# Memory rows transposed unscaled, and cached log gates loaded 64 keys to a partition

## The chip, the cores and the metric

One Trainium2 chip, one core of it. The kernel is one launch; its time is device microseconds (us) from start to end. Three runs give 1922.89, 1914.52 and 1916.93, median 1916.93. Engines by the names of the profile: PE is TensorE (matmuls), PEld its weight loads, DVE VectorE, ACT ScalarE, POOL GpSimd, SP SyncE, which issues all the transfers spoken of here.

## The reference

One step of a layer for 1,024 prompt frames and 8 decode streams of 16 new frames each, with 1,024 cached keys a stream. Three token mixers run side by side (stick-breaking attention, SSD, forgetting attention "fox"), then cross-attention into 256 memory rows and an FFN. The change touches two pieces:

```
def mem_kv(mem, g, wk, wv):
    mn = rmsnorm(mem, g)                       # mem (256, 1024): row * rsqrt(mean square) * gain of the column
    k = einsum('bmd,de->bme', mn, wk)          # 1024 x 1024, likewise v with wv
# forgetting attention of the decode streams
logf = log_sigmoid(fg + fox_b_f)               # gates of the new rows, 4 heads
fcum = cumsum(concat([past['fox_logf'], logf], axis=1), axis=1)    # past: (8, 1024, 4)
s = s + (fcum of the query - fcum of the key)  # added to the scores before the softmax
```

`p_mem_k`, `p_mem_v`, the new gates `p_fox_logf`, `s_fox_logf` and the outputs of the layer are returned.

## The kernel before

All large products are f32 by three passes: an operand is split into a high part (a cast on ACT, `split_into`) and a low part (the difference, usually on POOL in pieces of 256 columns, L132), and `mm3` (L325 to L328) adds high x high, high x low and low x high.

**Order of the work.** One program order per engine is fixed when the kernel is built: a scheduler simulates the engines and places each instruction where its operands would be ready, and `keep_in_program_order` pins some. On the chip each engine runs its list in that order and waits at an instruction whose operand is late; what stands behind it on that engine waits too. SP issues the transfers in such a list.

**Start.** L140 to L148 load the memory rows `xm` (two halves of 128 rows), five rows of gains and the convolution taps, and the first two blocks of `wk_x`. `norm_T` (L259 to L278) squares the rows on ACT (L265), takes the root (`rstd_of`), scales the rows in place on DVE (L269), transposes them on TensorE (L275) and copies the transposes out, with the gain of the column, as high (ACT, L276) and low part (DVE, L277). `mem_proj` then runs 16 units, each 256 rows of `wk_x` or `wv_x` by 512 columns: `w_unit` loads the block (L315), splits it (ACT cast L290, POOL L132), two units ahead; 12 products per unit (two row halves, two k tiles, three passes). After four units the sums go from PSUM to SBUF (ACT copy) and are stored twice (L835). Between the units a helper `aux` norms and transposes the prompt frames (loads L437, the same `norm_T` lines), whose products with `w_in` come next.

**`fox_sums`.** Lies some 280 us in, in the stream of filling work between attention units. It makes the new gates `lf` (a chain of small DVE instructions, L402 to L409, then L660), stores them (L662, L663), loads the cached gates with key p of each 128 on partition p (L666), sums the prompt's gates along the keys with a triangular matrix (L678, L679) and does the same for the cached gates: block sums on DVE (L693 to L696), 15 products with `triu` and `ones` into rows of (stream, head) (L708, L710), ACT copies, the new rows' sums behind them (L713 to L717). The rows go to a scratch `fs_sc` in DRAM, written twice (L718). Each of the four fox decode units later loads its gate rows from there, spread over the partitions (`fkb`, L909), and L1246 loads the column of the new rows.

Around `fox_sums` stand a decode unit of stick-breaking attention (key loads L882, their transposes L888, the weights made on POOL L132 and transposed at L925) and the blocks of `w_in` for the z and xBC columns (L315, cast L290, splits L132).

## Time and profile before

| what | value |
|---|---|
| median of three runs | 1916.93 us |
| profiled execution | 1915.89 us, span 1914.2 us |
| granted TensorE clock, mean | 0.988 |
| TensorE busy | 1837.6 us, 96% |
| DVE, ACT, POOL busy | 897.1, 823.7, 622.6 us |
| packets below 512 B | 89996 of 309742 |

A row of busy time adds up the time in which an engine worked; the span less TensorE's busy time is what TensorE stood. In a list of waits the line is that of the waiting instruction, behind "<-" stands what released it. In a timeline a row is: start and duration in us, engine, line, operation, tiles out and in, shapes, count, and in brackets the idle time of the engine ahead of it with its releaser. "clock" is the share of full speed that TensorE was granted.

### The profile page before, as it was taken

To read this page: it belongs to the slowest core of one execution; us is meant where nothing else is said; L and a number is where in the kernel's file an instruction comes from. 1 tells how busy PE (TensorE), PEld (TensorE's weight loads), DVE (VectorE), ACT (ScalarE), POOL (GpSimd) and SP (SyncE) were. 2 spreads that over 40 slices of the span, in tenths; PEclk is the share of its full clock that TensorE was granted. 3 is DMA by queue.
4 is the path that set the end of the run, shared out by engine and by line. 5 is a ranking of instruction groups with operands and counts; after the bars stand their busy time and mean duration, and the time that the engine had idled before them with its cause. 6 is when DMAs were issued, how large, how long until landed. Compare 5 with 4: busy or idle time off the path is not lost. (4 is left out here: it accounts for less than half of the span.)

```text
span 1914.2 us, 32508 instructions
## 1 busy us (share of the span) xinstructions
PE 1837.6 (96%) x12146; PEld 1641.4 (86%) x12146; DVE 897.1 (47%) x1823; ACT 823.7 (43%) x1782; POOL 622.6 (33%) x921
## 2 busy tenths in 40 slices
PE   7989989999998889999999999999999999999998
PEld 5889877888876667898998889999999999888886
DVE  3421323457646873353445387333333433455554
ACT  6431534545566771243433275333333333344443
POOL 7532416254324563211102205544444443000000
PEclk9999998999999999999999999999999999999999
DMA  9455645536579887244558124322323223567572
GB/s 336 142 165 159 211 115 152 154 109 185 166 220 282 280 290 260 103 150 145 176 194 291 66 91 111 80 70 70 95 74 75 70 70 100 190 194 237 177 246 92
DMA packets 309742, 305.70 MB, mean 160 GB/s; under 512 B 89996, under 2 KB 261108, under 8 KB 309584
## 3 DMA queue, kind: packets, MB, share of 16 engines
q1 hardware_dynamic: 309584, 303.62, 51.6%
q8 instruction: 96, 1.57, 0.3%
q14 instruction: 62, 0.51, 0.1%
HBM read 229.31 MB, written 74.24 MB: 159 GB/s over the span
## 5 line engine op out<-in xcount | busy, mean ns | idle before, releaser
L132 POOL TENSOR_TENSOR wl<-wr,wh 128x256 fp32r<-128x256 f32 (+2 forms) x184 | 138.6, 787 | 222.4 <-ACT wh L290 202.0
L326 PE MATMUL psd<-act,wh 128*128 128x384 f32 x576 | 198.7, 345 | 5.1 <-DVE sg L453 2.7
L327 PE MATMUL psd<-act,wh 128*128 128x384 f32 x576 | 197.6, 343 | 0.0
L328 PE MATMUL psd<-act,wl 128*128 128x384 f32 x576 | 196.8, 342 | 0.7 <-POOL wl L132 0.7
L1849 PE MATMUL pst<-bT,tr 128*128 128x256 f32 (+1 forms) x1068 | 155.0, 293 | 0.0
L1849 PEld LDWEIGHTS pst<-bT,tr 128*128 128x128 f32 x1068 | 144.9, 188 | 0.1
L328 PE MATMUL psd<-wh,act 128*128 128x512 f32 (+3 forms) x424 | 135.8, 322 | 0.0
L326 PE MATMUL psd<-wh,act 128*128 128x256 f32 (+3 forms) x414 | 133.0, 324 | 2.4 <-ACT pt L1445 1.2
L1849 PE MATMUL psd<-bT,tr 128*128 128x320 f32 (+1 forms) x912 | 133.2, 295 | 0.8 <-DVE tr L1693 0.5
L327 PE MATMUL psd<-wl,act 128*128 128x256 f32 (+3 forms) x414 | 132.8, 322 | 0.5 <-POOL wl L132 0.5
L1849 PEld LDWEIGHTS psd<-bT,tr 128*128 128x128 f32 x912 | 124.7, 188 | 1.8 <-DVE tr L1693 0.7
L326 PEld LDWEIGHTS psd<-act,wh 128*128 128x128 f32 x576 | 109.1, 189 | 8.7 <-DVE sg L453 3.1
L132 POOL TENSOR_TENSOR tr<-u,tr 128x256 fp32r<-128x256 f32 x110 | 81.9, 774 | 102.3 <-ACT tr L1689 85.1
L328 PEld LDWEIGHTS psd<-act,wl 128*128 128x128 f32 x576 | 108.9, 189 | 2.3 <-POOL wl L132 1.0
L327 PEld LDWEIGHTS psd<-act,wh 128*128 128x128 f32 x576 | 109.0, 189 | 1.5 <-issue 1.1
L132 POOL TENSOR_TENSOR ws<-ws 128x256 f32<-128x256 f32 (+2 forms) x100 | 68.5, 713 | 115.3 <-DVE ws L519 99.9
L1824 DVE TENSOR_TENSOR tr<-tr,pst 128x256 f32<-128x256 f32 (+1 forms) x86 | 38.6, 449 | 139.5 <-ACT tr L1821 106.3
L251 POOL TENSOR_SCALAR sm<-sm 128x1 f32<-128x1 f32 (+2 forms) x27 | 7.1, 261 | 296.6 <-ACT y L1932 208.0
L132 POOL TENSOR_TENSOR tr<-raw,tr 128x256 fp32r<-128x256 f32 x94 | 69.2, 765 | 84.5 <-ACT tr L1689 76.3
L1689 ACT CAST tr<-tr 128x384 fp32r<-128x384 f32 (+1 forms) x70 | 37.7, 538 | 121.1 <-DMA tr<-hidsc 104.3
L290 ACT CAST wh<-wr 128x512 fp32r<-128x512 f32 (+2 forms) x90 | 52.2, 621 | 80.7 <-PE psd L328 31.0
L326 PEld LDWEIGHTS psd<-wh,act 128*128 128x128 f32 x414 | 78.3, 189 | 9.9 <-ACT pt L1445 1.5
(620 smaller groups left out, 4714.0 us busy)
## 6 DMA issues: line engine op xcount, KB each, us to landing
u<-w_down SPq DMA_DIRECT2D x40, 512.0 KB
raw<-w_down SPq DMA_DIRECT2D x26, 512.0 KB
st<-qksc SPq DMA_DIRECT2D x48, 256.0 KB
wr<-w_in SPq DMA_DIRECT2D x44, 256.0 KB
tr<-hidsc SPq DMA_DIRECT2D x57, 192.0 KB
hidsc<-tr SPq DMA_DIRECT2D x34, 288.0 KB
qksc<-sg SPq DMA_DIRECT2D x48, 192.0 KB
wr<-cache_sb_k SPq DMA_DIRECT2D x32, 256.0 KB
```

What stands on the lines that cost most here:

```text
L132: POOL.tensor_tensor(out=out[:, a0:a1], in0=in0[:, a0:a1], in1=in1[:, a0:a1], op=op)
L251: POOL.tensor_scalar(v, ss, inv, EPS, ALU.mult, ALU.add)
L290: ACT.copy(hi, raw)
L326: PE.matmul(out, ah, bh, start=start, stop=False)
L327: PE.matmul(out, ah, bl, start=False, stop=False)
L328: PE.matmul(out, al, bh, start=False, stop=stop)
L1689: ACT.copy(hi, src)
L1824: DVE.tensor_tensor(out=at(out, g), in0=at(x, g), in1=ps[g][:, :GW[g]], op=op)
L1849: PE.matmul(dst[g][:, :GW[g]], x[:, ka], y[:, k, :], start=start and k == 0 and m == 0, stop=stop and k == 3 and m == 2, skip_group_check= ...
```

## The change

Three edits.

1. *Memory rows.* The rows are transposed as loaded; the copies out of PSUM apply only the gain. The squares and the root follow after the first unit (`root`), and the root of a memory row is applied when the products are copied out (scale `rstd[0]`, kept in `xm_r`). The loads are reordered: first half of the rows, five gain rows, second half, four blocks of `wk_x`, then the taps, which get their own transpose after the second unit (`tap_columns`). Weight blocks are loaded four units ahead, split two ahead as before; the low parts of 7 of 16 units (0, 1, 2, 5, 8, 11, 14) are made on DVE in one instruction, the others on POOL.
2. *Cached gates.* The load puts 64 consecutive keys of one stream on a partition (16 partitions a stream), all heads together: 128 runs of 1 KB where there were 8,192 of 16 bytes. Four scans on DVE, one a head, sum within a partition; one small product with a constant matrix `before` adds the partitions ahead of it. `fs_sc` is now (head, stream, key), written once; the sums of the new rows go to `fn_sc`.
3. *Gate rows.* Each fox decode unit loads its rows `fkb` by two transfers, one a stream.

On TensorE the instructions of the start come in another order. What stands in its list (`pst`, `psd`: PSUM tiles; `xc`: gain rows; `act`: memory rows and their transposes; `wh`, `wl`: high and low parts of the weights), before:

```order
L219 MATMUL pst<-ident,xc 128x72
L275 MATMUL pst<-ident,act 128x128 x6
L326 MATMUL psd<-wh,act 128x512
L327 MATMUL psd<-wl,act 128x512
L326 MATMUL psd<-wh,act 128x512
L327 MATMUL psd<-wl,act 128x512
L275 MATMUL pst<-ident,act 128x128 x2
```

and now:

```order
L226 MATMUL pst<-ident,xc 128x40
L843 MATMUL pst<-ident,act 128x128 x12
L340 MATMUL psd<-wh,act 128x512 x2
L341 MATMUL psd<-wl,act 128x512
L342 MATMUL psd<-wh,act 128x512
L340 MATMUL psd<-wh,act 128x512
L341 MATMUL psd<-wl,act 128x512
```

Twelve of the sixteen transposes stand ahead of the first product, where six did.

On SP, the loads of the start (`ws`: prompt frames; `hb`: small constants; `wr`: blocks of `w_in`; `st`: blocks of `wk_x`), before:

```order
L315 DMA st<-wk_x 128x2x512
L437 DMA ws<-x_prompt 128x1024 x3
L1220 DMA hb<-fox_b_f 128x4
L1221 DMA hb<-dt_bias 128x8
L1222 DMA hb<-a_log 128x8
L1223 DMA hb<-d_skip 128x8
L437 DMA ws<-x_prompt 128x1024 x4
L315 DMA wr<-w_in 128x4x128
L315 DMA st<-wk_x 128x2x512 x5
```

and now:

```order
L147 DMA st<-wk_x 128x2x512 x4
L156 DMA xc<-conv_w 32x128
L861 DMA st<-wk_x 128x2x512
L451 DMA ws<-x_prompt 128x1024 x3
L1265 DMA hb<-fox_b_f 128x4
L1266 DMA hb<-dt_bias 128x8
L1267 DMA hb<-a_log 128x8
L1268 DMA hb<-d_skip 128x8
L451 DMA ws<-x_prompt 128x1024 x4
L329 DMA wr<-w_in 128x4x128 x4
L861 DMA st<-wk_x 128x2x512 x3
```

Five blocks of `wk_x` go out ahead of the frames, where three did, and four blocks of `w_in` ahead of the sixth block, where one did.

On SP at `fox_sums` (`sg`: cached gates; `lf`: new gates), before:

```order
L666 DMA sg<-cache_fox_logf 128x64x4
L882 DMA wr<-cache_sb_k 128x512 x2
L608 DMA mixsc<-sg 64x2x256
L882 DMA wr<-cache_sb_k 128x512 x2
L662 DMA p_fox_logf<-lf 128x8x4
L663 DMA s_fox_logf<-lf 128x4
L315 DMA wr<-w_in 128x2x256
```

and now:

```order
L681 DMA sg<-cache_fox_logf 128x256
L927 DMA wr<-cache_sb_k 128x512 x2
L622 DMA mixsc<-sg 64x2x256
L927 DMA wr<-cache_sb_k 128x512 x2
L329 DMA wr<-w_in 128x2x256
L329 DMA wr<-w_in 128x2x8
L329 DMA wr<-w_in 128x2x256
L329 DMA wr<-w_in 128x2x8
L329 DMA wr<-w_in 128x2x256
L329 DMA wr<-w_in 128x2x8
L329 DMA wr<-w_in 128x2x256
L676 DMA p_fox_logf<-lf 128x8x4
L677 DMA s_fox_logf<-lf 128x4
L329 DMA wr<-w_in 128x2x8
```

The stores of `lf` moved behind seven of the eight `w_in` pieces. On DVE the four scans (L712) stand directly ahead of the first instruction of the chain that ends in `lf` (L416, before L402). Elsewhere the lists of all engines are as they were, but for the two loads of `fkb`.

The diff, cut to its core:

```diff
-    xm = act_t(F32)
-    for i in range(2):
+    xm, rows = act_t(F32), xc_t()
+    first_raw = []
+    def load_xm(i):
         SP.dma_start(out=xm[:, i * D:(i + 1) * D], in_=a["mem_prompt"][0, i * P:(i + 1) * P, :])
-    rows = xc_t()
+    def load_wk(n):
+        first_raw.append(st_t(F32))
+        SP.dma_start(out=first_raw[-1].rearrange("p (k n) -> p k n", n=512),
+                     in_=a["wk_x"][0][2 * n * P:(2 * n + 2) * P, 0:512].rearrange("(k p) n -> p k n", p=P))
+    load_xm(0)
     for i, g in enumerate(("norm_mix_g", "norm_x_g", "norm_ffn_g", "mem_norm_g", "conv_b")):
         SP.dma_start(out=rows[8 * i:8 * i + 8, :P], in_=a[g][0].rearrange("(k p) -> k p", p=P))
-    SP.dma_start(out=rows[40:72, :P], in_=a["conv_w"][0].rearrange("i (k p) -> (i k) p", p=P))
-    first_raw = []
-    for k0 in (0, 2):
-        first_raw.append(st_t(F32))
-        SP.dma_start(out=first_raw[-1].rearrange("p (k n) -> p k n", n=512),
-                     in_=a["wk_x"][0][k0 * P:(k0 + 2) * P, 0:512].rearrange("(k p) n -> p k n", p=P))
+    load_xm(1)
+    for n in range(4):
+        load_wk(n)
+    SP.dma_start(out=rows[64:96, :P], in_=a["conv_w"][0].rearrange("i (k p) -> (i k) p", p=P))
...
     colp = pT()
-    PE.transpose(colp[:, :72], rows[:72, :P], ident[:72, :72])
+    PE.transpose(colp[:, :40], rows[:40, :P], ident[:40, :40])
     cols = cst.tile([P, 72], F32, name="cols")
-    DVE.tensor_copy(cols, colp[:, :72])
-    DVE.tensor_scalar(cols[:, 32:72], cols[:, 32:72], 0.5, None, ALU.mult)
+    DVE.tensor_copy(cols[:, 0:40], colp[:, :40])
+    def tap_columns():
+        tp = pT()
+        PE.transpose(tp[:, :32], rows[64:96, :P], ident[64:96, 64:96])
+        DVE.tensor_copy(cols[:, 40:72], tp[:, :32])
+        DVE.tensor_scalar(cols[:, 32:72], cols[:, 32:72], 0.5, None, ALU.mult)
     g_mix, g_x, g_ffn, g_mem = (cols[:, 8 * i:8 * i + 8] for i in range(4))
...
     hb = mcst.tile([P, 28], F32, name="hb")
+    xm_r = mcst.tile([P, 2], F32, name="xm_r")
     lf = mcst.tile([P, NBLK, 4], F32, name="lf")
...
     fc_sc = dram([4, SEQ], F32, "fcsc")
-    fs_sc = dram([32, 2, PAST + DEC_S], F32, "fssc")
+    fs_sc = dram([4, DEC_B, PAST], F32, "fssc")
+    fn_sc = dram([32, DEC_S], F32, "fnsc")
     ac_sc = dram([72, P], F32, "acsc")
...
-    def split_unit(raw, n):
+    def split_unit(raw, n, eng=POOL):
         hi, lo = unit_pair()
-        split_into(hi[:, :n], lo[:, :n], raw[:, :n])
+        split_into(hi[:, :n], lo[:, :n], raw[:, :n], eng)
         return hi, lo
...
-        pl0, pl1 = sg_t(), sg_t()
-        SP.dma_start(out=pl0[:, :256].rearrange("p (u h) -> p u h", h=4),
-                     in_=a["cache_fox_logf"][0].rearrange("b k h -> (b k) h").rearrange("(u p) h -> p u h", p=P))
-        triu, ones = pl1[:, 256:384], pl1[:, 384:512]
-        POOL.memset(pl1[:, 256:], 1.0)
+        lp, tri = sg_t(), sg_t()
+        SP.dma_start(out=lp[:, :256], in_=a["cache_fox_logf"][0].rearrange("b (c k) h -> (b c) (k h)", k=64))
+        triu, ones, before = (tri[:, i * P:(i + 1) * P] for i in range(3))
+        POOL.memset(tri[:, :384], 1.0)
         POOL.affine_select(out=triu, in_=triu, compare_op=ALU.is_ge, fill=0.0, base=0, pattern=[[1, P]],
                            channel_multiplier=-1)
+        b3 = before.rearrange("p (b t) -> p b t", t=16)
+        POOL.affine_select(out=b3, in_=b3, compare_op=ALU.is_ge, fill=0.0, base=-1, pattern=[[16, 8], [1, 16]],
+                           channel_multiplier=-1)
+        POOL.affine_select(out=b3, in_=b3, compare_op=ALU.is_ge, fill=0.0, base=0, pattern=[[-16, 8], [0, 16]],
+                           channel_multiplier=1)
...
         DVE.tensor_copy(fqc.rearrange("p b h -> p (b h)"), tp[:, :32])
-        pp, ps_ = pl1[:, :256], pl0[:, 256:]
-        DVE.tensor_copy(pp.rearrange("p (k b h) -> p k b h", k=8, h=4),
-                        pl0[:, :256].rearrange("p (b k h) -> p k b h", k=8, h=4))
         yield
...
         SP.dma_start(out=fc_sc, in_=fr[0:4, :SEQ])
-        DVE.tensor_copy(ps_[:, 32:64], pp[:, 0:32])
-        for k in range(1, 7):
-            sl = slice(32 * k, 32 * k + 32)
-            DVE.tensor_tensor(out=ps_[:, 32 * k + 32:32 * k + 64], in0=ps_[:, sl], in1=pp[:, sl], op=ALU.add)
-        x8 = sg2_t()
-        DVE.tensor_tensor(out=x8[:, :32].rearrange("p (b h) -> p b h", h=4),
-                          in0=lf[:, 8, :].unsqueeze(1).to_broadcast([P, 8, 4]),
-                          in1=smask.unsqueeze(2).to_broadcast([P, 8, 4]), op=ALU.mult)
+        for hd in range(4):
+            x = lp[:, hd:256:4]
+            DVE.tensor_tensor_scan(lp[:, 256 + 64 * hd:320 + 64 * hd], x, x, 0.0, ALU.add, ALU.bypass)
+        tot = pre[:, 32:36]
+        DVE.tensor_copy(tot, lp[:, 319:512:64])
+        x8, t8 = pre[:, 64:96], pre[:, 96:128]
+        for out, src in ((x8, lf[:, 8, :]), (t8, tot)):
+            DVE.tensor_tensor(out=out.rearrange("p (b h) -> p b h", h=4), in0=src.unsqueeze(1).to_broadcast([P, 8, 4]),
+                              in1=smask.unsqueeze(2).to_broadcast([P, 8, 4]), op=ALU.mult)
         yield
-        sr = xc_t()[0:32, :PAST + DEC_S]
-        for hf in range(2):
-            tp = pd()
-            for k in range(4 * hf, 4 * hf + 4):
-                o = tp[:32, (k % 4) * P:(k % 4 + 1) * P]
-                PE.matmul(o, pp[:, k * 32:(k + 1) * 32], triu, start=True, stop=k == 0)
-                if k:
-                    PE.matmul(o, ps_[:, k * 32:(k + 1) * 32], ones, start=False, stop=True)
-            ACT.copy(sr[:, hf * 512:(hf + 1) * 512], tp[:32])
         tp = pd()
-        PE.matmul(tp[:32, :16], x8[:, :32], fold, start=True, stop=True)
-        ACT.copy(x8[0:32, 64:80], tp[:32, :16])
-        n8 = x8[0:32, 64:80]
+        PE.matmul(tp[:, :4], before, tot, start=True, stop=True)
+        PE.matmul(tp[:32, 16:32], x8, fold, start=True, stop=True)
+        PE.matmul(tp[:32, 32:48], t8, ones[:, :16], start=True, stop=True)
+        DVE.tensor_tensor(out=lp[:, 256:512].rearrange("p (h k) -> p h k", h=4),
+                          in0=lp[:, 256:512].rearrange("p (h k) -> p h k", h=4),
+                          in1=tp[:, 0:4].unsqueeze(2).to_broadcast([P, 4, 64]), op=ALU.add)
+        n8 = pre[0:32, 128:144]
+        DVE.tensor_copy(n8, tp[:32, 16:32])
         DVE.tensor_tensor_scan(n8, n8, n8, 0.0, ALU.add, ALU.bypass)
-        DVE.tensor_scalar(sr[:, PAST:], n8, sr[:, PAST - 1:PAST], None, ALU.add)
-        SP.dma_start(out=fs_sc, in_=sr.unsqueeze(1).to_broadcast([32, 2, PAST + DEC_S]))
+        DVE.tensor_tensor(out=n8, in0=n8, in1=tp[:32, 32:48], op=ALU.add)
+        SP.dma_start(out=fs_sc.rearrange("h b (c k) -> (b c) h k", k=64),
+                     in_=lp[:, 256:512].rearrange("p (h k) -> p h k", h=4))
+        SP.dma_start(out=fn_sc, in_=n8)
         yield
...
         DVE.tensor_tensor(out=y8[0:32, :P].rearrange("p (b t) -> p b t", t=DEC_S),
-                          in0=sr[:, PAST:].unsqueeze(1).to_broadcast([32, 8, DEC_S]),
+                          in0=n8.unsqueeze(1).to_broadcast([32, 8, DEC_S]),
                           in1=bmask32.unsqueeze(2).to_broadcast([32, 8, DEC_S]), op=ALU.mult)
...
         mh, ml = act_pair(256)
-        drain(norm_T([xm[:, i * D:(i + 1) * D] for i in range(2)], g_mem, lambda: (mh, ml), 256, xm[:, 2 * D:]))
         work = [(a[wname][0], j, k0, sc, out) for wname, sc, out in (("wk_x", mk_sc, "p_mem_k"), ("wv_x", mv_sc, "p_mem_v"))
                 for j in range(2) for k0 in (0, 2, 4, 6)]
-        nxt = [[t[:, :1024].rearrange("p (k n) -> p k n", n=512) for t in split_unit(raw, 1024)] for raw in first_raw]
+        def unit(n):
+            return [t[:, :1024].rearrange("p (k n) -> p k n", n=512)
+                    for t in split_unit(first_raw.pop(0), 1024, DVE if n < 2 or n % 3 == 2 else POOL)]
+        nxt = [unit(0)]
+        for k in range(KT):
+            tp = pT()
+            for i in range(2):
+                PE.transpose(tp[:, i * P:(i + 1) * P], xm[:, i * D + k * P:i * D + (k + 1) * P], ident)
+            ACT.activation(mh[:, k, :], tp[:, :256], AF.Copy, scale=g_mem[:, k:k + 1])
+            DVE.scalar_tensor_tensor(ml[:, k, :], tp[:, :256], g_mem[:, k:k + 1], f32(mh[:, k, :]), ALU.mult, ALU.subtract)
+        nxt.append(unit(1))
+        ss, rstd = small(2), []
+        def root():
+            for i in range(2):
+                tc.keep_in_program_order(ACT.activation(xm[:, 2 * D:], xm[:, i * D:(i + 1) * D], AF.Square,
+                                                        accum_out=ss[:, i:i + 1]))
+            r = xm_r[:, 0:2]
+            DVE.tensor_copy(r, rstd_of(ss, 2, 1.0 / D))
+            rstd.append(r)
         for n, (w, j, k0, sc, out) in enumerate(work):
             wh, wl = nxt.pop(0)
-            if n + 2 < len(work) :
-                w2, j2, k2 = work[n + 2][:3]
-                nxt.append(w_unit([(w2, j2 * 512, 512)], k2, 2, st_t(F32)))
+            if n + 4 < len(work):
+                w2, j2, k2 = work[n + 4][:3]
+                first_raw.append(st_t(F32))
+                SP.dma_start(out=first_raw[-1].rearrange("p (k n) -> p k n", n=512),
+                             in_=w2[k2 * P:(k2 + 2) * P, j2 * 512:(j2 + 1) * 512].rearrange("(k p) n -> p k n", p=P))
+            if n + 2 < len(work):
+                nxt.append(unit(n + 2))
             if k0 == 0:
...
                     t = sg_t()
-                    ACT.copy(t, ps[i])
+                    ACT.activation(t, ps[i], AF.Copy, scale=rstd[0][:, i:i + 1])
                     for dst in (sc, a[out][0, 0].rearrange("m h d -> m (h d)")):
                         SP.dma_start(out=dst[i * P:(i + 1) * P, j * 512:(j + 1) * 512], in_=t)
+            if n == 0:
+                root()
+            if n == 1:
+                tap_columns()
             next(aux, None)
...
             fkb = xc_t()
-            SP.dma_start(out=fkb[:, :PAST],
-                         in_=fs_sc[8 * p:8 * p + 8, :, :PAST].rearrange("i c k -> (i c) k").unsqueeze(1)
-                         .to_broadcast([16, DEC_S // 2, PAST]))
+            for b2 in range(2):
+                SP.dma_start(out=fkb[64 * b2:64 * b2 + 64, :PAST],
+                             in_=fs_sc[:, 2 * p + b2, :].unsqueeze(1).to_broadcast([4, DEC_S, PAST]))
             return fox_rows(T, pieces, [(0, PAST, fkb[:, :PAST]), (PAST, P, fnew)], fqs[:, p:p + 1]), hold
...
                     tc.keep_in_program_order(
-                        SP.dma_start(out=fqs[:, p:p + 1], in_=fs_sc[8 * p:8 * p + 8, 0, PAST:PAST + DEC_S]))
+                        SP.dma_start(out=fqs[:, p:p + 1], in_=fn_sc[8 * p:8 * p + 8, :]))
             if o[0] == "z":
...
             elif o == "dt":
```

## The prediction

> **What bounds the kernel now.** I read the page's busy shares first, then its chain, then TensorE's waits, and last the timeline and stretches around the two longest.
>
> ```profile
> span 1914.2 us, 32508 instructions
> PE 1837.6 (96%) x12146; PEld 1641.4 (86%) x12146; DVE 897.1 (47%) x1823; ACT 823.7 (43%) x1782; POOL 622.6 (33%) x921
> PE 45%; DVE 1%; issue 0%; POOL 0%; ACT 0%; DVEq 0%; POOLq 0%
> ```
>
> TensorE is busy for 96% of the span; 76.6 us are idle. So only two things shorten the run: fewer products, or a shorter stop of TensorE. The chain says the same (DVE, POOL and ACT have a hundredth or less of the span). The profiled execution took 1915.89 us, 1.7 more than its span and 1.0 less than the median of the three runs (1916.93); sums below start from 1915.9, and I leave the 1.0 out, as the three runs lie 8.4 apart.
>
> The waits of TensorE (line, for whom; total us, times, longest):
>
> ```profile
> PE pst L219 <- DMA xc<-conv_w: 7.0, 1, 7.0
> PE pst L888 <- DMA wr<-cache_sb_k: 5.8, 4, 4.9
> PE pst L925 <- POOL ws L132: 3.5, 1, 3.5
> PE pst L275 <- DVE act L277: 1.2, 2, 0.9
> PE psd L327 <- POOL wl L132: 0.5, 1, 0.5
> ```
>
> The first, fourth and fifth lie in the memory projection at the start, the second and third around `fox_sums`. Stretches of those two places (us, then busy us of PE, PEld, DVE, ACT, POOL; clock granted to TensorE, DMA share, GB/s):
>
> ```profile
> 0.00:10.00 10.00, 0.37 (x2) 0.20 (x2) 6.05 (x37) 4.78 (x7) 4.99 (x21) 1.00 0.75 253
> 17.00:34.00 17.00, 15.81 (x82) 12.33 (x81) 8.97 (x18) 11.77 (x22) 9.14 (x15) 1.00 1.07 375
> 280.00:285.00 5.00, 0.09 (x5) 0.03 (x1) 3.47 (x20) 1.09 (x2) 0.60 (x2) 0.73 1.03 130
> 285.00:292.50 7.50, 6.95 (x32) 6.07 (x33) 1.28 (x10) 2.36 (x5) 0.00 (x0) 0.50 0.81 153
> 292.50:300.50 8.00, 8.00 (x71) 5.78 (x69) 2.56 (x1) 7.29 (x16) 7.30 (x10) 1.00 0.93 258
> 300.50:305.00 4.50, 1.00 (x7) 0.53 (x8) 3.34 (x5) 1.87 (x6) 4.50 (x7) 0.75 0.90 277
> 305.00:308.50 3.50, 3.50 (x15) 3.11 (x14) 0.42 (x1) 1.69 (x4) 2.16 (x6) 0.50 0.07 17
> ```
>
> At the start the DMA engines are full from 17 to 34 us. Around `fox_sums` TensorE stops twice, and behind each stop it works for a while at a clock of 0.50.
>
> **Part 1, the memory projection.** Timeline of the start (start, duration, engine, line):
>
> ```profile
> 4.18 1.06 ACT L265 ACTIVATE act<-act 128x1024 f32<-128x1024 f32 x1 [2.11 <-DMA act<-mem_prompt]
> 7.53 1.05 ACT L290 CAST wh<-st 128x1024 fp32r<-128x1024 f32 x1 [0.70 <-DMA st<-wk_x]
> 8.61 2.45 DVE L269 TENSOR_SCALAR act<-act,sm 128x1024 f32<-128x1024 f32 x2
> 12.16 0.80 PE L326 MATMUL psd<-wh,act 128*128 128x512 f32 x1
> 33.48 0.40 PE L328 MATMUL pss<-wh,act 128*128 128x512 f32 x1
> 33.71 0.62 PE L326 MATMUL pss<-wh,act 128*128 128x512 f32 x2
> 36.48 0.63 PE L326 MATMUL pss<-wh,act 128*128 128x512 f32 x2
> ```
>
> Before, the first product (12.16) waits for square, root, scaling (2.45 on DVE) and transposes. After, the transposes need only the rows; their copies are scaled by the gain. The second half of the rows is now issued behind five gain rows (about 0.3 us each on SP), so I put its arrival near 6.2; the first weight block still lands about 7.5 and is cast by 9.0; the first product of high parts can run at 9.2, **3.0 earlier**.
>
> That gain is not kept, I think, since the weights come no faster than the queue delivers. The sixth unit's block is issued behind two memory halves, seven frame-row blocks, four `w_in` blocks and five weight blocks: 1.05 + 3.67 + 1.05 + 2.62 MB, and its own 0.52, 8.9 MB. At 253 GB/s for the first 10 us (2.5 MB) and 375 after, it lands 17.1 us later, at 27.1, with about 1.2 for the landing at 28.3. The cast takes until 30.0 with ACT's other work. For the split:
>
> ```profile
> L1693 DVE TENSOR_TENSOR tr<-tr 128x384 fp32r<-128x384 f32 x51 | 28.5, 558 | 101.8 <-ACT tr L1689 94.3 <-PE pst L327 4.8 <-PE psd L1849 2.7
> L1693 DVE TENSOR_TENSOR tr<-u,tr 128x512 fp32r<-128x512 f32 x64 | 42.5, 689 | 5.1 <-ACT tr L1689 3.4 <-PE pss L327 0.6 <-PE pst L327 0.4
> L132 POOL TENSOR_TENSOR wl<-st,wh 128x256 fp32r<-128x256 f32 x64 | 48.3, 793 | 8.6 <-ACT wh L290 8.4
> ```
>
> DVE takes about 1.0 ns more for each column (131 ns for 128), so a block of 1,024 costs 1.2 us, against 4 x 0.79 = 3.2 on POOL. That ends at 31.2. The unit's twelve products, 0.23 apart as 33.48 and 33.71 show, end at 33.7, where before they run from 33.71 to 36.48: **-2.8**. The 0.5 that TensorE later waits for a split by POOL (psd L327 above) goes as well, because DVE now makes seven of the sixteen splits. Sum **-3.3**. Bounds: -1.0, when the loads for the frames starve the weights further; -4.7, when all of the 3.0 is kept with the 1.2 of L277 and the 0.5. I take the value between, by the sum of bytes. DVE's seven splits (8.4 us) replace 3.2 us of squares on ACT no longer waited for and 2.5 of scaling; DVE has 9 of 17 us busy there, so they cost nothing; without that slack, 8.4 - 2.5 = 5.9. The taps' transpose and the two copies after unit 1 cost some 0.4 inside the same slack.
>
> **Part 2, the cached gates.** Timeline of that place, and the DMA packets from 277.5 to 283.5:
>
> ```profile
> DMA packets 8373, 0.31 MB, mean 52 GB/s; under 512 B 8224, under 2 KB 8344, under 8 KB 8373
> 277.54 5.25 SPq L882 DMA_DIRECT2D wr<-cache_sb_k  x2
> 282.50 0.20 DVE L660 SCALAR_TENSOR_TENSOR lf<-lf,sg 128x36 f32<-128x36 f32 x1
> 285.00 1.94 PE L888 MATMUL pst<-ident,wr 128*128 128x128 f32 x8 [4.91 <-DMA wr<-cache_sb_k]
> 286.12 5.14 SPq L315 DMA_DIRECT2D wr<-w_in  x8
> 292.48 0.63 ACT L290 CAST wh<-wr 128x528 fp32r<-128x528 f32 x1 [1.66 <-DMA wr<-w_in]
> 293.20 8.52 POOL L132 TENSOR_TENSOR wl<-wr,wh 128x256 fp32r<-128x256 f32 x12 [9.76 <-PE pst L577]
> 301.72 4.58 POOL L132 TENSOR_TENSOR ws<-ws 128x256 f32<-128x256 f32 x5
> 304.73 1.13 PE L925 MATMUL pst<-ident,ws 128*128 128x128 f32 x4 [3.50 <-POOL ws L132]
> ```
>
> The gate load is 8,192 packets of 16 bytes, and they are nearly all the packets of six microseconds (52 GB/s). The keys stand behind them, SP is held for 5.25 us, and the `w_in` blocks start at 286.12. From there one chain leads to the second stop: last `w_in` landed, cast (292.48), POOL's splits (293.20, 8.52 long), POOL's attention weights (301.72), TensorE's transposes of them (304.73).
>
> After, 128 packets of 1 KB carry the same 0.13 MB, about 1 us at 130 GB/s; it lands at 279.3, the keys at 280.2. But the four scans now stand on DVE ahead of the chain that makes the new gates `lf`:
>
> ```profile
> L519 DVE TENSOR_TENSOR_SCAN ws<-ws 128x1152 f32<-128x1152 f32 x1 | 2.6, 2557 | 8.7 <-ACT ws L516 8.7
> L519 DVE TENSOR_TENSOR_SCAN ws<-ws 128x128 f32<-128x128 f32 x4 | 2.7, 663 | 0.6 <-ACT ws L516 0.6
> ```
>
> and of the products that go, two pieces of the timeline:
>
> ```profile
> 295.29 0.38 PE L710 MATMUL psd<-sg 128*32 128x128 f32 x2
> 295.51 0.38 PE L708 MATMUL psd<-sg 128*32 128x128 f32 x2
> ```
>
> (2557 - 663) / 1024 is 1.85 ns a column, so 64 columns take 0.55 us, four 2.2; with the strided source I take 2.4, and 0.2 of waiting for the load. `lf` is then ready at 285.3 instead of 282.7. TensorE passes the key transposes at 280.4 and stands about 2.1 before the product that needs `lf`. The first stop shrinks from 4.9 to some 2.6.
>
> The second stop decides. Seven of the eight `w_in` pieces are issued before SP waits for `lf`; the last, of 8 columns, is issued behind the two gate stores, at 286.5, and lands at 289.5. ACT casts in order, so the last cast and the sigmoids behind it end at 290.4. POOL starts on the earlier casts at 284 and has its twelve pieces done at 293.1 (it waits for the last pieces). Then come about 3.0 of pieces of weights, until TensorE can go on: 296.2 against 304.73, **-8.5**. TensorE's own work would get there at 295.2: 280.4 + 2.1 + (6.95 + 8.00 + 1.00 busy in the three stretches, less 3.3). So it waits 1.0, and POOL's chain has the word. Those 3.3 are the thirty products that go (two each 0.22, by the last two rows); they are priced at nothing because they lie ahead of that wait, and would be worth up to 3.3 if POOL were earlier.
>
> Behind it stand 3.50 busy us at a clock of 0.50, which would be 1.75 at full clock. With a stop of 1.0 in the place of 3.5 I take half of that, **-0.9**. Sum of this part **-9.4**. Bounds: -5.2, SP's stall alone; -13, when POOL and the clock both give all (-8.5 - 1.75 and most of the 3.3).
>
> [...]
>
> **Part 3, the fox units.** The gate rows of each of the four decode units come by two loads:
>
> ```profile
> 520.17 0.68 SPq L909 DMA_DIRECT2D xc<-fssc  x1
> ```
>
> Four more issues on SP cost about 0.6 each, 2.2 in all. They are hidden by TensorE's work and the early request (a unit ahead); uncovered they would be that 2.2. Value 0. The stores of 256-byte packets lie more than 200 us ahead of the first reader.
>
> **Sum.** 1915.9 - 3.3 - 9.4 = 1903.2, forecast **1903**, own range 1899 to 1907.
>
> **The rivals.**
>
> R1, the chain of `w_in` moves by less. If the last small piece is later than I think, behind the stores that wait for `lf`, only SP's 5.2 comes back: 1915.9 - 3.3 - 5.2 = 1907.4. For it: ACT casts in order, and the piece of 8 columns has no other way. Against: seven of eight are issued early, and POOL can work on them. 0.17.
>
> R2, the start is starved. Frame rows and `w_in` blocks stand ahead of later weight blocks in a full queue (1.07 of the engines' time); the part gives -1.0: 1915.9 - 1.0 - 9.4 = 1905.5. Against: by the sum of bytes the sixth block's split ends 2.5 ahead of 33.71, where its products stood before. 0.13.
>
> R3, the clock holds and the last piece is not late. If it lands 2.5 us earlier, with the seven others, the weights are ready before TensorE and the stop is gone: another 2.5 and 0.85, 1899.8. For it: the clock rows; against: the scans ahead of `lf`. 0.12.
>
> R4, **slower**: the two loads of gate rows in each fox unit hold SP as the gate load does now. SP was held 5.25 us there, TensorE stopped 4.9, and then ran 6.95 busy us at a clock of 0.50, 3.5 more than at full clock. If the keys of each of the four units came that much later and TensorE's lead over them is used up, that is 5.25 + 3.5 a unit, 35 in all: 1915.9 - 12.7 + 35 = 1938. From 3.2 us a unit on (12.7 / 4) it turns the sign. Against: the packets are 4 KB, and SP issues eight `w_in` loads in 5.14, 0.64 each, without waiting. 0.06. [...]
>
> R5, the change does not do what it says: the 1 KB packets are no quicker, or SP is held by something else than the gate load; then only part 1 is left, about 1912. 0.05.
>
> **How the numbers follow.** Forecast 0.47, rivals 0.53. The range 1897 to 1912 takes in R1, R2, R3 and R5's centre, and leaves out R4 and the far sides of the bounds, about 2 in 10. A measurement of this kernel can tell 0.5% from no change, 9.6 us, so faster means below 1907.4. The forecast, R3 and most of R2 fall there, with a part of R1 on its edge: 0.70. Within: the rest of R1 and R2, R5 and a part of the forecast's spread, 0.24. Slower: R4, 0.06.
>
> **What would show it.** Part 1: the first product near 9 us, the sixth unit ending near 34, no wait for L132 by the products. Part 2: no stall of 5 us on SP at the gate load; the wait for the keys below 1 us, one near 2 for `lf` in its place; the wait of the weight transposes near 1 and the stretch behind it at a clock above 0.50. Part 3: waits of the fox units as before. I am wrong if the wait for POOL keeps 3 us or more while the first goes, if the memory projection ends less than 2 us earlier, or if TensorE waits for keys in the fox units.

## The result, and the profile after

The changed kernel is **slower**: median 1934.91 us (1930.29 to 1936.70, 6 runs) against 1914.78 for the kernel before (6 runs of the same sessions), ratio 1.0093, interval 1.0073 to 1.0114. The forecast was 1903 (own range 1899 to 1907, with the rivals 1897 to 1912). The profiled execution took 1935.84 us, 19.95 more than that of the kernel before.

The page of the changed kernel: span, busy shares, and the chain that ended last.

```profile
span 1934.1 us, 32440 instructions
PE 1846.6 (95%) x12121; PEld 1647.1 (85%) x12121; DVE 900.0 (47%) x1830; ACT 823.1 (43%) x1779; POOL 606.8 (31%) x895
PE 79%; DMA 8%; POOL 4%; DVE 3%; ACT 3%; issue 2%; SPq 1%; POOLq 0%; DVEq 0%; ACTq 0%
```

TensorE has 25 fewer instructions in the records and is busy 9 us longer, at a mean granted clock of 0.984 where it was 0.988; its idle time went from 76.6 us to 87.5. In the chain, transfers now hold 8% of the span, where before every part but TensorE was 1% or less. Its longest waits, and that for the stick-breaking keys (line, for whom; total us, times, longest):

```profile
PE pst L933 <- DMA wr<-cache_fox_k: 6.7, 1, 6.7
PE psd L340 <- DVE sg L430: 6.2, 1, 6.2
PE pss L573 <- ACT ws L531: 5.4, 6, 1.6
PE pst L970 <- POOL ws L132: 5.3, 3, 4.9
PE pst L226 <- DMA xc<-conv_b: 5.3, 1, 5.3
PE pst L933 <- ACT kf L935: 5.3, 3, 4.3
PE pst L933 <- DMA wr<-cache_sb_k: 2.4, 3, 1.7
```

The wait for the stick-breaking keys fell from 5.8 us to 2.4 (the longest from 4.9 to 1.7), the way of the forecast, which had it below 1. The wait for POOL's weights did not fall to 1 but rose to 4.9. The many short waits for ACT at L573 add up to 5.4, where those of the same line before (L559) made 1.4. And three stops of 6.7, 6.2 and 4.3 us are new. To see where they lie, one takes instructions that stand at the same place in both programs. First the timeline of the kernel before at four of them (the first frame product with its wait, the first z product, the last step ahead of the fox units, the first product behind them):

```profile
90.17 0.44 PE L326 MATMUL psd<-act,wh 128*128 128x384 f32 x1 [0.89 <-DVE sg L453]
310.25 0.39 PE L326 MATMUL psd<-wh,act 128*128 128x264 f32 x1
491.77 0.27 PE L760 MATMUL psd<-ident,so 128*27 128x128 f32 x1 [0.99 <-DVE so L756]
730.75 0.50 PE L326 MATMUL psd<-wh,ws 128*128 128x512 f32 x1 [0.84 <-DVE sg L1157]
```

and of the changed kernel:

```profile
87.83 0.44 PE L340 MATMUL psd<-act,wh 128*128 128x384 f32 x1 [0.89 <-DVE sg L467]
303.51 0.57 PE L340 MATMUL psd<-wh,act 128*128 128x264 f32 x1
489.45 0.27 PE L776 MATMUL psd<-ident,so 128*27 128x128 f32 x1 [1.29 <-DVE so L772]
745.60 0.50 PE L340 MATMUL psd<-wh,ws 128*128 128x512 f32 x1 [0.84 <-DVE sg L1202]
```

The start gains 2.3 us. By the first z product it is 6.7, so `fox_sums` added 4.4. By 491 us those 4.4 are given back (2.3 remain). Between 491 and 731 us, where the four fox decode units run, 17.2 are lost: from -2.3 to +14.9. TensorE stands 12.1 us longer there (34.4 for 22.4) and works 5.1 longer, at a mean clock of 0.95 where it was 0.98. The remaining 5 or so come behind that (below).

The loss is in the part that the prediction priced at nothing. The timeline of the first fox unit, in the kernel before:

```profile
525.66 1.15 ACT L529 ACTIVATE ws<-xc,fqs 128x1024 f32<-128x1024 f32 x1 [3.97 <-DMA xc<-fssc]
```

and in the changed one:

```profile
517.67 1.53 SPq L955 DMA_DIRECT2D xc<-fssc  x2
529.76 1.15 ACT L543 ACTIVATE ws<-xc,fqs 128x1024 f32<-128x1024 f32 x1 [10.29 <-DMA xc<-fssc]
532.37 0.58 PE L340 MATMUL psd<-wh,act 128*128 128x256 f32 x1 [6.21 <-DVE sg L430]
607.20 0.45 PE L933 MATMUL pst<-ident,wr 128*128 128x128 f32 x1 [6.72 <-DMA wr<-cache_fox_k]
```

The one load of gate rows was issued by 520.85 (520.17 and 0.68, the row in the prediction) and ACT could use it at 525.66, 4.8 later. The two half loads were issued by 519.20 and ACT waits for them until 529.76, 10.6 later. ACT takes its instructions in order, so the gates that it reads out of PSUM behind that wait (L429) are late, with them DVE (L430), and TensorE stands 6.2 us for a free PSUM tile. SP was not held here: 1.53 us for two issues. It is the transfer itself that is slow.

In the later units the slow loads hold others up. The load of the third unit, in the kernel before and then its second half in the changed one, with the key loads behind that, and a cast of ACT in the fourth unit:

```profile
583.69 0.55 SPq L909 DMA_DIRECT2D xc<-fssc  x1
```

```profile
593.65 4.94 SPq L955 DMA_DIRECT2D xc<-fssc  x1
602.01 6.63 SPq L927 DMA_DIRECT2D wr<-cache_fox_k  x2
654.93 0.36 ACT L463 CAST sg<-pso 64x256 fp32r<-64x256 f32 x1 [5.67 <-DMA mixsc<-sg]
```

In the third unit SP is held in the issue itself. From the issue of the gate rows to the end of that of the five key loads behind them pass 16.1 us, where it was 11.3 before, and TensorE stands 6.7 us for keys (607.20 above). In the fourth, ACT waits 5.7 us for a store, by the order on SP one that was issued behind the two half loads; its copies of keys come late, and that is the stop of 4.3.

A stretch of the first unit in which little else is under way, before and after (columns as in the prediction; the last three are clock, DMA share and GB/s):

```profile
521.90:523.40 1.50, 1.50 (x15) 1.50 (x14) 1.43 (x5) 0.00 (x0) 1.50 (x6) 1.00 0.97 300
```

```profile
520.00:521.90 1.90, 1.90 (x20) 1.90 (x18) 0.62 (x4) 0.00 (x0) 1.90 (x7) 1.00 0.32 87
```

With the old load under way the 16 DMA engines are busy for 0.97 of the time; with the new ones for a third of it, at 87 GB/s.

### The profile page after: what moved, and what is told of

It is laid out like the page before. It is cut to its first block, busy times and chain, and to the rows that moved or that the text cites. A ratio compares the mean times of both kernels' runs of the same rounds, so it can differ in the third digit from the quotient of the medians.

```text
span 1934.1 us, 32440 instructions
## 1 busy us (share of the span) xinstructions
PE 1846.6 (95%) x12121; PEld 1647.1 (85%) x12121; DVE 900.0 (47%) x1830; ACT 823.1 (43%) x1779; POOL 606.8 (31%) x895
## 4 chain that ended last, share of the span: by engine, by line
PE 79%; DMA 8%; POOL 4%; DVE 3%; ACT 3%; issue 2%; SPq 1%; POOLq 0%; DVEq 0%; ACTq 0%
PE psd L1894 11%; PE psd L340 10%; PE psd L341 10%; PE psd L342 9%; PE pst L1894 8%; PE pss L1894 4%; PE pss L340 3%; PE pss L341 3%; PE pss L342 3%; PE pso L1894 2%; POOL wl L132 2%; PE pst L340 1%; PE pst L341 1%; PE pst L342 1%; DMA act<-acsc 1%
## 5 line engine op out<-in xcount | busy, mean ns | idle before, releaser
L132 POOL TENSOR_TENSOR wl<-wr,wh 128x256 fp32r<-128x256 f32 (+2 forms) x184 | 141.0, 802 | 224.8 <-ACT wh L304 213.1
L132 POOL TENSOR_TENSOR tr<-u,tr 128x256 fp32r<-128x256 f32 x110 | 82.6, 779 | 100.9 <-ACT tr L1734 83.0
L132 POOL TENSOR_TENSOR ws<-ws 128x256 f32<-128x256 f32 (+2 forms) x100 | 70.1, 729 | 116.5 <-DVE ws L533 103.1
L132 POOL TENSOR_TENSOR tr<-raw,tr 128x256 fp32r<-128x256 f32 x94 | 69.2, 765 | 85.2 <-ACT tr L1734 77.0
L340 PEld LDWEIGHTS psd<-wh,act 128*128 128x128 f32 x414 | 80.0, 194 | 16.0 <-DVE sg L430 6.4
L342 PEld LDWEIGHTS psd<-wh,act 128*128 128x128 f32 x424 | 82.0, 193 | 6.3 <-issue 0.4
```

What stands on the lines that cost most here:

```text
L132: POOL.tensor_tensor(out=out[:, a0:a1], in0=in0[:, a0:a1], in1=in1[:, a0:a1], op=op)
L340: PE.matmul(out, ah, bh, start=start, stop=False)
L342: PE.matmul(out, al, bh, start=False, stop=stop)
```

## The experiments

Executions of one kernel scatter here by up to 9 us to either side of their median, so below 1% only an interval says anything. In a table at the end of this section stand the start times of the four instructions above in each profiled execution.

**Fox loads from 16 rows.** A load of the changed kernel reads 4 rows of the scratch (one a head), each to 16 partitions: a pattern of 4 x 16 x 1024, with the 4 outermost. Here the sums are stored in copies, so that the outermost number can be raised while the number of loads, their size and, but for the added stores, the order on the engines stay:

```diff
-    fs_sc = dram([4, DEC_B, PAST], F32, "fssc")
+    fs_sc = dram([4, 4, DEC_B, PAST], F32, "fssc")
...
-        SP.dma_start(out=fs_sc.rearrange("h b (c k) -> (b c) h k", k=64),
-                     in_=lp[:, 256:512].rearrange("p (h k) -> p h k", h=4))
+        for c in range(4):
+            SP.dma_start(out=fs_sc[:, c].rearrange("h b (c k) -> (b c) h k", k=64),
+                         in_=lp[:, 256:512].rearrange("p (h k) -> p h k", h=4))
...
-                             in_=fs_sc[:, 2 * p + b2, :].unsqueeze(1).to_broadcast([4, DEC_S, PAST]))
+                             in_=fs_sc.rearrange("h c b k -> (h c) b k")[:, 2 * p + b2, :].unsqueeze(1)
+                             .to_broadcast([16, 4, PAST]))
```

> The changed kernel, but the gate sums are stored four times, so that each of the two loads of a fox unit reads 16 different rows, each to 4 partitions, where the changed kernel reads 4 rows, each to 16 partitions. The order of all engines stays, but for three more stores far from the fox units. Theory S (spread): the loads are slow because their outermost dimension has 4 entries and only 4 of the 16 DMA engines carry them; with 16 the loads land some 6 us after their issue as before the change, the three long stops in the fox units (6.2, 6.7, 4.3 us) go, and the time falls by about 20 us, to 1914 to 1917. Theory N (number of issues): two loads in the place of one hold SP and the queue; the time stays at 1932 to 1937. Theory R (repeats): 16 reads of one row are slow; also 1914 to 1917.

Measured: 1909.48 us (10 runs) against 1914.08, ratio 0.9973, interval 0.9951 to 0.9995. That is 25 us below the median of the changed kernel. Theory N falls: there are still two loads a unit. It is some 5 us below the range that theories S and R named (a second measurement, below, gives 1913.2). In the trace the key loads of the third unit are issued 10.3 us behind the gate rows, and the three long stops are gone: none between 485 and 735 us is longer than 2.2.

The traces also show that TensorE, ACT and DVE run the first fox unit in another order in the changed kernel than before (from 528 to 550 us in the trace of the kernel before), which the list of differences ahead of the prediction does not name. This kernel and the next have the new order too, so the order is not what costs the 17 us.

**Fox loads from 8 rows**, the same with two copies ([8, 8, PAST]).

> As the last, with two copies: each load reads 8 different rows, each to 8 partitions (as often as the kernel before read a row). Theory S: 8 DMA engines, a load takes twice as long as with 16 and half as long as with 4; DMA share near 0.5 while nothing else is queued; time between, 1915 to 1924. Theory R: 8 repeats were fast before, so it equals the run with four copies. Theory N: 1932 to 1937.

Measured: 1921.48 us (10 runs), ratio 1.0037 (1.0018 to 1.0056). So 4, 8 and 16 outermost entries give 1934.9, 1921.5 and 1909.5. Theory R falls too: with 8 reads of each row, as many as in the kernel before, the time is 12 us above the run with 16 rows (8 above its second measurement), clear of the intervals. The first unit's stretch and ACT's wait with 8 rows:

```profile
521.30:523.30 2.00, 2.00 (x20) 2.00 (x19) 0.57 (x4) 0.00 (x0) 2.00 (x8) 1.00 0.45 123
519.16 1.49 SPq L956 DMA_DIRECT2D xc<-fssc  x2
527.51 1.15 ACT L543 ACTIVATE ws<-xc,fqs 128x1024 f32<-128x1024 f32 x1 [6.86 <-DMA xc<-fssc]
```

and with 16:

```profile
520.00:521.50 1.50, 1.50 (x15) 1.50 (x14) 0.07 (x2) 0.00 (x0) 1.50 (x6) 1.00 0.78 214
517.48 1.39 SPq L956 DMA_DIRECT2D xc<-fssc  x2
523.30 1.15 ACT L543 ACTIVATE ws<-xc,fqs 128x1024 f32<-128x1024 f32 x1 [4.41 <-DMA xc<-fssc]
```

DMA share 0.32, 0.45, 0.78 and rate 87, 123, 214 GB/s for 4, 8 and 16; the wait of ACT 10.3, 6.9, 4.4 us. The share and the rate are those of all transfers and hold some other packets too, so they are not the load's alone. The records of the single packets count it more directly. These loads move in packets of 4 KB. While the first unit's load runs, mostly four such packets are under way at a time in the changed kernel (520.2 to 526.6 us), six to eight with 8 rows (521.0 to 524.4), up to 16 with 16 rows, and some 16 in the kernel before.

**Many loads of one row.** One store, and eight loads a unit, each of one row to 16 partitions:

```diff
-                SP.dma_start(out=fkb[64 * b2:64 * b2 + 64, :PAST],
-                             in_=fs_sc[:, 2 * p + b2, :].unsqueeze(1).to_broadcast([4, DEC_S, PAST]))
+                for hd in range(4):
+                    r0 = 64 * b2 + 16 * hd
+                    SP.dma_start(out=fkb[r0:r0 + 16, :PAST],
+                                 in_=fs_sc[hd, 2 * p + b2:2 * p + b2 + 1, :].to_broadcast([DEC_S, PAST]))
```

> The changed kernel with one store, and eight loads a fox unit: each reads one row to 16 partitions (16 repeats, outermost dimension 16). The order of the engines shifts a little around the fox units. Theory S: fast landing, as with four copies, less about 4 us of SP issue time a unit that may or may not be hidden: 1914 to 1922. Theory R: slow, 1930 or more. Theory N: slower than the changed kernel, 1937 or more.

Measured: 1931.76 us (4 runs), ratio 1.0094 (1.0070 to 1.0119). The size that only theory R had named; theory S, with 1914 to 1922, missed it. But the trace shows the opposite of R's mechanism:

```profile
519.50 1.97 SPq L957 DMA_DIRECT2D xc<-fssc  x4
524.27 1.15 ACT L543 ACTIVATE ws<-xc,fqs 128x1024 f32<-128x1024 f32 x1 [2.14 <-DMA xc<-fssc]
```

With 16 reads of each row the last load, a quarter as large as those of the changed kernel, is usable 2.8 us after its issue, sooner than in any other kernel. The first fox unit does not lose; the loss of 17 us is made up of many smaller stops between 560 and 700 us, the longest of 4.1 and 3.9, at a mean clock of 0.90. This kernel has 24 more issues on SP than the changed one (in the third unit three of them hold SP for 6.01 us) and another order around these units. Which of the two costs the time was not separated. So in these runs the loads of 4 and of 8 rows are slow (usable 10.6 and 6.9 us after their issue, 4.4 with 16), and many loads are no way out.

**Part 3 alone**, on the kernel before, from its own scratch:

```diff
-            SP.dma_start(out=fkb[:, :PAST],
-                         in_=fs_sc[8 * p:8 * p + 8, :, :PAST].rearrange("i c k -> (i c) k").unsqueeze(1)
-                         .to_broadcast([16, DEC_S // 2, PAST]))
+            for b2 in range(2):
+                SP.dma_start(out=fkb[64 * b2:64 * b2 + 64, :PAST],
+                             in_=fs_sc[8 * p + 4 * b2:8 * p + 4 * b2 + 4, 0, :PAST].unsqueeze(1)
+                             .to_broadcast([4, DEC_S, PAST]))
```

> The kernel before with only the loads of the gate rows changed: two loads a fox unit, each of 4 rows to 16 partitions, from its own scratch. Theory S and theory R: the whole loss of the fox units comes alone, +18 to +22 us on the kernel before, 1933 to 1937. Theory N the same. If instead the loss needs the earlier arrival or the new order of parts 1 and 2, it is less than +5.

Measured: 1934.30 us (4 runs), ratio 1.0098 (1.0067 to 1.0129): the whole loss, without parts 1 and 2. ACT waits 10.9 us for the first rows, and TensorE again 6.8 and 7.7 us behind it.

**Part 1 alone**: the hunks of the diff on the loads at the start, the memory rows and the split on DVE, nothing of `fox_sums` or the fox units.

> The kernel before with part 1 alone (memory rows, order of the loads at the start, seven low parts on DVE). The trace of the changed kernel has TensorE 2.5 us ahead from 86 us on. Theory A (kept): nothing later gives it back, -2 to -3 us on the kernel before. Theory B (given back at the first stop that a transfer or POOL sets, near 285 or 305 us): within 1 us of the kernel before.

Measured: 1922.29 us (12 runs) against 1913.20, ratio 1.0041 (1.0026 to 1.0057). Neither theory: it is slower. The profiled execution, 1913.93, was the shortest of the twelve, so two more were profiled.

> Part 1 alone once more, for its trace: its timed executions had a median of 1922.3 us, its profiled one took 1913.9. Theory L (lost at the start): in an execution of the usual length TensorE is behind the kernel before already at 86 us. Theory F (lost later): it is ahead by 0.4 to 2.5 us at 86 us and falls behind where cached rows are loaded, between 280 and 760 us.

> The same kernel a third time, with the same expectations, so that two executions of the usual length can be laid beside the short one.

Measured: 1920.57 and 1917.62. All three are 0.2 to 0.4 us ahead at 90 us, and 3.3, 4.7 and 4.1 behind at 492. So theory F. The place is a stop of 3.0 us near 402 us, which the three have and the kernel before has not:

```profile
PE psd L773 <- DVE so L769: 3.0, 1, 3.0
```

The scheduler, with part 1 alone in the program, puts the instructions of all four engines between some 320 and 405 us in another order. The changed kernel does not have this order: between 330 and 528 us its engines run the list of the kernel before. So what part 1 alone costs here is not a cost of part 1 in the changed kernel. By 731 us 3.0 to 4.7 of that have come back, and what makes the median 9 us longer was not found in these traces. The twelve timed executions ran on another chip than the two further ones, which was not separated.

**Part 2 alone**, with the fox loads from 16 rows.

> The kernel before with part 2 alone, with the fox loads over 16 rows (gate sums stored four times). Theory: the stop for the keys goes, the stop for POOL's weights grows from 3.5 to about 5 us with a longer cold stretch behind it, so part 2 is worth only -1 to -3 us and not the 9.4 of the forecast. If the forecast's size was right and something else hid it, -8 or more.

Measured: 1912.18 us (12 runs), ratio 0.9991 (0.9978 to 1.0005): nothing that can be told from no change, within the -1 to -3 expected, and far from the 9.4 of the forecast. The stop for POOL's weights is 4.9 in its trace, as expected.

**The stores of the new gates later**, on the kernel with 16 rows: the two stores of `lf` moved from `fox_sums` to the place of the `fqs` loads, near 510 us.

> The kernel with the fox loads over 16 rows, and the two stores of the new gates moved from between the seventh and the eighth piece of w_in to the place near 510 us where the sums of the new rows are loaded. Theory Q (the last piece waits behind the stores): the last cast comes 1.1 us earlier, the stop for POOL's weights falls from 4.9 to about 3.8, and the time is 1 to 2 us lower than with the stores where they were. Theory V (POOL is held by the scans of DVE, whenever it starts): the stop stays above 4.5 and the time moves by less than 1 us.

Measured: 1914.37 us (12 runs), ratio 1.0007 (0.9993 to 1.0020). The last cast, with the stores where they were (16 rows) and then with the stores later:

```profile
288.81 0.63 ACT L304 CAST wh<-wr 128x528 fp32r<-128x528 f32 x1 [2.12 <-DMA wr<-w_in]
```

```profile
285.49 0.63 ACT L304 CAST wh<-wr 128x528 fp32r<-128x528 f32 x1 [0.52 <-DMA wr<-w_in]
283.66 9.53 POOL L132 TENSOR_TENSOR wl<-wr,wh 128x256 fp32r<-128x256 f32 x11
287.30 2.61 DVE L533 TENSOR_TENSOR_SCAN ws<-ws 128x1152 f32<-128x1152 f32 x1 [0.61 <-ACT ws L530]
290.25 2.25 DVE L533 TENSOR_TENSOR_SCAN ws<-ws 128x896 f32<-128x896 f32 x1
```

The piece was late behind the stores indeed, by more than thought: the cast comes 3.3 earlier, 1.7 when the better start of that execution (1.6) is taken off. But the stop for POOL's weights is 5.4, not 3.8: POOL, fed in time, now takes 9.53 for its eleven pieces, because the last ones lie under the scans all the same. The first z product starts at 301.41 instead of 303.31, of which 1.6 is that start. Theory V holds, theory Q is right on the transfer and wrong on the stop.

**And the second half of the z block split on DVE**:

```diff
-        u1 = w_unit(srcs, 4, 4)
+        u1 = w_unit(srcs, 4, 4, eng=eng)          # eng is DVE for the z block with dt
```

> As the last, and the low parts of the second half of the z block of w_in (four pieces of 256 and two of 16 columns on POOL) are made on DVE in two instructions. Theory V: POOL has no pieces left that the scans can hold ahead of the attention weights; the stop falls below 2.5 us, the cold stretch behind it shortens, and the time is 3 to 6 us below the kernel with 16 rows alone. Theory D (DVE is the bound there): the scans come later by the two splits (1.2 us) and the stop keeps its 4 to 5 us; no gain.

Measured: 1913.81 us (12 runs), ratio 1.0004 (0.9991 to 1.0018). Two answers. TensorE's waits for POOL's weights between 290 and 330 us are, with 16 rows alone and then in this kernel:

```profile
PE pst L972 <- POOL ws L132: 4.9, 1, 4.9
```

```profile
PE pst L970 <- POOL ws L132: 2.8, 2, 1.6
PE psd L775 <- DVE so L771: 3.0, 1, 3.0
```

So theory V is right on the stop: it goes from one of 4.9 to 1.6 and 1.2, and the first z product starts 9.0 us before that of the kernel before. But the time does not follow. By 492 us the lead is 0.8; the other row is a stop of 3.0 near 397 us, the same that part 1 alone has. From some 355 to 405 us the two kernels have the same order on all four engines, and the kernel with 16 rows has another. So this run shows what sets the stop, and does not show what its removal would be worth in the order of the changed kernel.

**The kernel with 16 rows once more**, as a candidate that beats both:

> The changed kernel with fox loads over 16 rows once more, in five rounds, as the version that may beat both: its ratio to the kernel before was 0.9973 (0.9951 to 0.9995), while two kernels that differ from it by small moves came out at 1.0007 and 1.0004. If the first ratio holds: 0.995 to 0.999. If it was the scatter of a few us from execution to execution: 0.999 to 1.002.

Measured: 1913.23 us (12 runs) against 1914.52, ratio 0.9999 (0.9985 to 1.0014). The first gain is not confirmed (the two intervals overlap from 0.9985 to 0.9995): with its load mended the change is not shown to be worth anything. No version here is shown to beat the kernel before.

Start times of the four instructions, as differences to the kernel before (us; one profiled execution each):

| kernel | 90.17 | 310.25 | 491.77 | 730.75 | median, ratio |
|---|---|---|---|---|---|
| the change | -2.3 | -6.7 | -2.3 | +14.9 | 1934.9, 1.0093 |
| part 3 alone | +0.2 | +1.5 | +2.9 | +22.1 | 1934.3, 1.0098 |
| loads of one row | -2.3 | -6.4 | -4.7 | +12.6 | 1931.8, 1.0094 |
| 8 rows | -0.2 | -5.6 | -1.1 | -0.7 | 1921.5, 1.0037 |
| 16 rows | -0.7 | -6.9 | -2.9 | -5.9 | 1909.5, 0.9973 |
| 16 rows, again | -1.6 | -5.1 | -0.7 | -7.5 | 1913.2, 0.9999 |
| part 2, 16 rows | -0.6 | -4.8 | -1.6 | -5.2 | 1912.2, 0.9991 |
| stores later | -2.3 | -8.8 | -4.9 | -9.0 | 1914.4, 1.0007 |
| and z split on DVE | -1.4 | -9.0 | -0.8 | -3.7 | 1913.8, 1.0004 |
| part 1 (three executions) | -0.2, -0.4, -0.4 | -2.7, -1.6, -0.8 | +3.3, +4.7, +4.1 | -1.4, +1.7, +0.6 | 1922.3, 1.0041 |

Between the third and the fourth column lie the fox units: +17 and +19 with 4 rows, +17 with loads of one row, +0.5 with 8, -3 to -7 with 16. Every row with part 2 shows a gain at 310, and a part of it, from 1.7 to 8.2 us, gone by 492. Part 2 alone leaves the start as it was and still has -0.6 at 90, so differences of that size there mean nothing. A single execution's last column may lie several us from its kernel's median; only the jumps from column to column are read here.

## Why the prediction was wrong

It failed twice: part 3 cost 20 us where it was priced at nothing, and the 12.7 forecast for parts 1 and 2 did not reach the end of the program, as the kernel with 16 rows shows (ratios 0.9973 and 0.9999, where 1903 would be 0.993).

**Part 3 is the larger failure.** The step reads "Four more issues on SP cost about 0.6 each ... Value 0". It costed the issues and took the transfer for unchanged, because the bytes were. It cost 17 us in the fox units, and 20 on its own. The order of the dimensions had changed: 16 outermost before, 4 after, and in the runs the packets under way at a time follow this number (four, six to eight, up to 16 for 4, 8, 16), and with them the rate (87, 123, 214 GB/s) and ACT's wait (10.3, 6.9, 4.4 us).

From 520.4 to 521.6 us of the changed kernel, with four of the 4 KB packets under way and little else, the DMA share is 0.26, about 4 of the 16 engines by their time. Which engines took the packets the traces do not show.

**R4 had the side and a part of the mechanism.** It let the two loads hold SP in every unit, and put 35 us on it. In the first unit they did not (1.53 us for both): what was late were the rows themselves, and behind them, on ACT and DVE in their order, the PSUM tiles that TensorE needed. In the third unit they did (4.94 us, and 6.63 for the keys behind), and TensorE waited 6.7 us for keys, the sign of being wrong that the prediction named. With 16 rows the second half's issue in that unit still takes 3.53, but the keys follow in time (no wait for them above 1.4 there). What neither R4 nor the forecast had is why: the transfer is slow. Its chance of 0.06 came from looking at SP alone.

**Part 1** came out near its sum in the profiled execution, 2.3 of 3.3: the first product at 9.47 (forecast 9.2), no wait of a product for L132 at the start, the cast of the sixth block at 30.82 (ended by 30.0 in the forecast). In other executions with part 1 the gain is 0.2 to 2.3, so R2's size is nearer the truth in some. R2's mechanism is not what the trace shows: no product waits for a weight. TensorE stops at 28.71 and 30.58 us for the copies of the frames' transposes (1.1 and 0.3), and from 30.5 to 34 us its clock is 0.56 and then 0.50, where it was 1.00 before; that is 1.6 us of work at full speed, a term that the prediction does not have. So in this run stops much shorter than the 4.91 and 3.50 of the prediction's rows were followed by a clock of 0.50, and to count on a higher one behind a stop of 1.0 was not safe.

**Part 2: the first stop shrank, the second did not.** The changed kernel at that place:

```profile
274.77 0.88 SPq L927 DMA_DIRECT2D wr<-cache_sb_k  x2
276.38 0.84 DVE L712 TENSOR_TENSOR_SCAN sg<-sg 128x64 f32<-128x64 f32 x4 [0.80 <-DMA sg<-cache_fox_logf]
278.45 4.55 SPq L329 DMA_DIRECT2D wr<-w_in  x7
284.26 0.43 SPq L329 DMA_DIRECT2D wr<-w_in  x1
289.01 0.63 ACT L304 CAST wh<-wr 128x528 fp32r<-128x528 f32 x1 [2.55 <-DMA wr<-w_in]
289.72 5.57 POOL L132 TENSOR_TENSOR wl<-wr,wh 128x256 fp32r<-128x256 f32 x3 [1.49 <-ACT wh L304]
289.85 3.02 DVE L533 TENSOR_TENSOR_SCAN ws<-ws 128x1152 f32<-128x1152 f32 x1 [2.62 <-ACT ws L530]
298.76 0.49 PE L970 MATMUL pst<-ident,ws 128*128 128x128 f32 x1 [4.93 <-POOL ws L132]
299.00:303.00 4.00, 4.00 (x22) 3.83 (x22) 1.30 (x4) 0.98 (x3) 4.00 (x9) 0.50 0.43 97
303.00:306.00 3.00, 3.00 (x16) 3.00 (x15) 0.76 (x1) 1.15 (x3) 3.00 (x6) 0.50 0.19 44
```

TensorE is 2.8 ahead at this place (its last key transposes ahead of it start at 273.28 for 276.03), so 2.8 is added to compare with the forecast's times. SP's stall of 5.25 is gone (0.88). The scans take 0.84 together and not 2.4, so the stop for `lf` did not come. The last cast ends at 292.4 where the forecast had it done by 290.4, 2.0 later. And POOL needs 5.57 for the last three pieces, where the sum left 2.7 from the last cast to their end: two of them lie under DVE's scans of 1152 and 896 columns and end 0.52 and 0.02 behind them, after 2.99 and 1.93 us. TensorE goes on at 301.6, not at 296.2. The trace of the kernel before has the same in it (last section): its 8.52 for twelve pieces hold 3.0 for one piece under a scan. The prediction read them as one link of its chain and did not name the scan. The forecast of a stop of 1.0 became one of 4.9, and the clock behind it stays at 0.50 for seven us and not for 3.5. What a stop of 1.0 would leave of that stretch (the forecast's 0.9, R3's further 0.85) was the author's estimate, which no run shows; with the z block split on DVE, where the stops were 1.6 and 1.2, the clock was 0.50 from 299 to 303 us and 0.63 in the 4 us behind. That is the term that was mis-sized: -4.4 for -9.4. R1, with -5.2, had the sum about right at that point; the late last piece that it named is 2.0 of the delay of 5.4, and POOL's pieces are the rest. That POOL's pieces set the stop is shown by the run that took the last of them off POOL; that the late last piece alone does not is shown by the run with later stores.

**Then it is given back.** At 398 us TensorE waits 2.0 us for POOL in the changed kernel; in the kernel before it waits 1.3 for ACT and 0.7 for POOL with work between. The stretch behind it, in the changed kernel and then in the kernel before:

```profile
398.00:402.00 4.00, 3.92 (x16) 3.93 (x17) 3.23 (x5) 2.79 (x7) 1.97 (x4) 0.67 0.38 139
402.00:406.00 4.00, 4.00 (x23) 3.23 (x23) 0.63 (x2) 0.51 (x2) 1.71 (x4) 0.91 0.34 131
```

```profile
402.00:406.00 4.00, 3.75 (x22) 3.76 (x23) 3.23 (x5) 2.94 (x7) 1.97 (x4) 1.00 0.45 142
```

The clock falls after the one wait and not after the two; 4 us at 0.67 and 4 at 0.91 are 1.7 us of work at full speed. Followed by the same instructions in both traces, the lead is 6.7 at the first z product and 5.2 two us later (the clock is still 0.50, where it was 1.00 before); 4.3 at 326 us, behind two stops for ACT (0.4 and 1.4); 5.4 at 400 and 2.7 at 405. The prediction had followed the gain only to the first z product.

**Behind the fox units** another 5.1 are lost, 1.8 of it waiting for rows of the mixers (749.76 us) and 1.1 at a wait for ACT near the end (2.2 at 1673.65, 1.1 before); the kernel with 16 rows loses 4.4 there in its first trace and 1.1 in its second. What puts them there stays open, as does why part 1 alone has a median 9 us up, when its three profiled executions lie -2.0, +4.7 and +1.7 from that of the kernel before.

## What to carry to other kernels

For each transfer that a change rewrites, compare the access pattern and not only the bytes: here the packets under way at a time went with the outermost dimension of the source (four, six to eight, up to 16 for 4, 8, 16), and a broadcast of 4 rows ran at 87 GB/s where one of 16 ran at 214. A change that is worth 1% has to be followed to the end of the program, above all where a scheduler orders it: here most of the gain in front of 310 us was gone 180 us later in the changed kernel, and one part of the change, built alone, came with an order that the whole does not have. And a step priced at nothing deserves the same look as the largest term, at the landing of a transfer and at who waits in order behind it.
